# Output projection of a hybrid decoder block: eight quarter products replaced by seven half products, with their sums made by transfers

## The chip, the core and the metric

The kernel runs on one core of one Trainium2 chip. The metric is the device time of one execution in microseconds (us), the median of several runs. All tiles are float32; matrix products are made from pairs of a rounded high part and a low remainder, three matmuls for one product of tiles.

The engines are named as the profile names them: PE (matmuls; PEld is its weight load), DVE (the vector engine), ACT (the scalar engine), POOL (GpSimd) and SP (the queue from which nearly all transfers are issued). Each engine takes its instructions in order.

## What is computed

One decoder block over a sequence of 1024 tokens with a model width of 1024. The part that the change rewrites is the output projection `y @ w_out`:

```
y = sigmoid(g_a) * (o_a @ w_o_swa) + sigmoid(g_b) * (o_b @ w_o_mla)
x = x + y @ w_out
h = rmsnorm(x, ffn_norm_g)
x = x + (silu(h @ w_gate) * (h @ w_up)) @ w_down
return rmsnorm(x, final_norm_g)
```

Here `o_a` and `o_b` are the outputs of a windowed attention and of a causal attention with eight heads each.

## The kernel before

The kernel runs through stages, each bound to PE. First come the norm and the input projections, the windowed attention with the gate products, and the causal attention (64 steps of one head and one block of 128 queries). In step t, PE makes the scores of step t + 2 and the transposes of the probabilities of step t; between the two, DVE masks (L1204), ACT takes the exponent into `p` (L1205) and POOL inverts the denominator `denb` (L1206) and scales `p` (L1207). In gaps of this order PE makes the product with `w_o_swa` (`mix_a`, tiles `oA`).

Then `mix_b` makes `o_b @ w_o_mla` into PSUM tiles `oB`, eight blocks of 128 columns of y with two halves of the sequence each. For each, ACT takes the sigmoids, POOL multiplies the first gate with its product (L1442), DVE multiplies `oB` with the second gate (L1428), adds the two into the tile `sg` (L180, `add`), and `split` (L163 on ACT, L166 on DVE) makes the high part `yh` and the low part `yl` in four pairs of tiles ("quads").

The output projection follows (loop `seg`). It runs over four quarters of the output: rows 0 to 511 left, rows 0 to 511 right, rows 512 to 1023 right, rows 512 to 1023 left. A quarter has four blocks of 128 rows, a block takes eight tiles of 128 along the inner dimension, and each of these takes the three matmuls of `mm3` (L172, L173, L174) with 512 columns into a PSUM tile `xo`. DVE adds the PSUM tile to the residual `x`. `w_out` is loaded in units of 128 x 1024 (`wr`) and split into `wv` (or `wh`, `wl`), four units for a quarter, the right half once for two quarters.

Of the rows that are complete, ACT takes the sum of squares (L1652), POOL the factor `rstd` (L311, L314), and DVE the scaled rows `xn` (L1657). PE transposes them (`to_h`, tiles `tp`), and ACT and DVE make from them the operands `b11`, `b21`, `b22`, `t1` to `t4` of the feed-forward stage, which already uses a scheme of seven half products for one of eight (class `Seven`: of two matrices cut into quarters, sums of quarters are formed, seven products of halves are made instead of eight, and the results are combined; `Seven.mix` and `Seven.prep` make its weight sums). Its products go to PSUM tiles `fa` and `fb`. The last stage is the down projection (`fd`).

Who stands where in an engine's queue is decided by the program: under `tc.manual_schedule` the named engines keep the order in which the code is written; outside it a scheduler orders them. SBUF tiles of 4 KB a partition come from a pool `U` of 21, those of 8 KB from a pool `V` of 17; PSUM tiles come from two pools of four banks (`P1` and `PX`). A tile that is asked for waits until the oldest of its pool is free.

Of the kernel before, what the change touches and what calls it, by code (L numbers as in the profile page):

```python
# [89 lines left out]
def hybrid_block_kernel(  # L90
# [208 lines left out]
    for dp in range(4):  # L299
        plain(("oa", dp), w_o_swa[dp], (P, 4, 256), True)  # L300
    for dp in (2, 0, 3, 1):
        plain(("ob", dp), w_o_mla[dp], (P, 4, 256))
    OUT0 = (2, 0, 3, 1)
    for r, hf in enumerate((0, 1, 0)):
        for j in (range(4) if r else OUT0):
            plain(("out", r, j), w_out[hf, j], (P, 2, 512), (r, j) != (2, 3))


# [722 lines left out]
    for it in range(N_SW):  # L1031
        if it + 2 < N_SW:
            sw_q(it + 2)
        gate_step()
        if it + 1 < N_SW:
            sw_qT(it + 1)
        sw[it].pop("norm")()
        gate_step()
# [245 lines left out]
    def mix_a(dc, sh, c0, n, ps=None):  # L1284
# [3 lines left out]
        if (sh, c0) == (0, 0):  # L1288
            if dc < 4:
# [9 lines left out]
        if c0 + n == 4:  # L1299
            nc.scalar.copy(ar[dc][:, half(sh)], oa_ps.pop((dc, sh)))  # L1300
            if sh == 1 and dc < 4:
                nc.sync.dma_start(ar_d[dc], ar.pop(dc))
# [16 lines left out]
    DCS = (4, 5, 0, 1, 6, 7, 2, 3)  # L1319

    def load_sigs(dc):
        for i in (dc, 8 + dc):
            load_sig(i)
        if dc < 4:
            ar[dc] = U("ar")
            nc.sync.dma_start(ar[dc], ar_d[dc])
# [35 lines left out]
    units = [(u // 2, u % 2, c) for u in range(16 - 3) for c in (0, 2)]  # L1362
# [4 lines left out]
    pvq = []  # L1367
    for t in range(NT):
# [20 lines left out]
        if t == NT - 1:  # L1389
            mix_a(13 // 2, 13 % 2, 0, 4, PX("oA"))  # L1390
        transposes(t)
        held[0] = True
# [5 lines left out]
        if t + 6 in w_at or t == 0:  # L1398
            st.load_to(st.index[("oa", w_at.get(t + 6, 0))])
# [6 lines left out]
        if e in (2, 6):  # L1406
            st.load_to(st.index[("ob", 2 if e == 2 else 0)])
        if e == 6:
            st.conv_to(st.index[("ob", 2)])
        held[0] = False  # L1410
    rest = [(i // 2, i % 2) for i in range(14, 16)]
# [6 lines left out]

    def mix_b(dc, i):
# [3 lines left out]
        ga, gb = gate.pop(dc), gate.pop(8 + dc)  # L1423
        for sh in range(2):
# [4 lines left out]
            if i == 7:  # L1429
                add(ga[:, cs], ga[:, cs], gb[:, cs], nc.vector)  # L1430
                split(*hT(dc, cs), ga[:, cs])
        for sh in range(2 if i < 7 else 0):
            cs = half(sh)
            add(ga[:, cs], ga[:, cs], gb[:, cs], nc.vector)
            split(*hT(dc, cs), ga[:, cs])
# [14 lines left out]
    st.conv_to(st.index[("ob", 0)])  # L1450
    new_quads("y")
    for i, dc in enumerate(DCS):
        if i in (1, 2):
            st.load_to(st.index[("ob", (3, 1)[i - 1])])
        if 2 <= i < 6:
            st.load_to(st.index[("out", 0, OUT0[i - 2])])
# [4 lines left out]
        if i + 1 < 8:  # L1461
            sigmoids(DCS[i + 1])
        mix_b(dc, i)
        if i in (1, 3):
            st.conv_to(st.index[("ob", (3, 1)[i // 2])])
        if i >= 4:
            st.conv_to(st.index[("out", 0, OUT0[i - 4])])

# [3 lines left out]
    x2 = {}  # L1472
# [3 lines left out]
    def to_h(xn, b):  # L1476
# [3 lines left out]
        for kh in range(2):  # L1480
            ps = PX("tp", (P, 4, P))
# [16 lines left out]
        t23 = U("t23", F32, (P, 2, 4, P))  # L1498
        sub(r[:, 0], pss[0], r[:, 0], nc.vector)
        nc.scalar.copy(t23[:, 1], pss[0])  # L1500
        sub(t23[:, 0], pss[1], r[:, 0], nc.vector)
        nc.scalar.copy(hq["t2"][0][:, :, blk(c)], t23[:, 0])
        sub(r[:, 1], r[:, 1], t23[:, 0], nc.vector)
        late.append((c, r))

        def rest():
            sub(t23[:, 1], pss[1], t23[:, 1], nc.vector)
            nc.scalar.copy(hq["b22"][0][:, :, blk(c)], pss[1])
            nc.scalar.copy(hq["t3"][0][:, :, blk(c)], t23[:, 1])  # L1509
            for name, src in (("t2", t23[:, 0]), ("b22", pss[1]), ("t3", t23[:, 1])):  # L1510
                hi, lo = hq[name]
                sub(lo[:, :, blk(c)], src, hi[:, :, blk(c)].bitcast(F32), nc.vector)
# [102 lines left out]

    in_order = tc.manual_schedule(engines={engines.PE, engines.DVE, engines.Activation, engines.Pool})
    prev = None
    late_parts = []
    for seg, (sh, hf) in enumerate(((0, 0), (0, 1), (1, 1), (1, 0))):
        if seg == 3:  # L1620
            in_order.__enter__()
        if seg in (0, 1, 3):
            r = {0: 0, 1: 1, 3: 2}[seg]
            wo2 = [st.get(("out", r, j)) for j in range(4)]
        hs = half(hf)
        for b in range(4 * sh, 4 * sh + 4):
            if seg in (0, 2):
                x2[b] = load_x(b)
            if (seg, b) == (2, 4):
                ffn.load_part(0, 0)  # L1630
            if (seg, b) == (2, 6):
                ffn.load_part(0, 1)
            if (seg, b) == (2, 7):
                ffn.mix(0)
            if seg == 0 and b < 2:
                if b == 0:
                    xo2 = [P1("xo") for _ in range(2)]
                    for ks in (DCS[:6], DCS[6:]):
                        for u in range(2):
                            mm3(xo2[u], [(hT(k, blk(u)), (wo2[k // 2][0][:, k % 2], wo2[k // 2][1][:, k % 2])) for k in ks],  # L1640
                                ks[0] == DCS[0], ks[0] != DCS[0])
                ps = xo2[b]
            else:
# [249 lines left out]
```

## Time and profile before

| what | value |
|---|---|
| time of the kernel, median of 3 runs | 1337.02 us (1336.59 to 1338.35) |
| time of the profiled execution | 1336.93 us |
| its span, first to last instruction | 1335.1 us |
| PE busy | 1323.6 us, 99% |
| DVE, ACT, POOL busy | 904.6, 636.5, 567.0 us |
| granted clock of PE over the span | 0.998 |

The span lies 1.8 us below the time of its own execution, which lies 0.1 us below the median. The profile's times are counted from the span's start. The first matmul of the output projection starts at 603.9 us, its last at 696.1 us.

### The profile page before, as it was taken

To read this page: it belongs to the slowest core of one execution; us is meant where nothing else is said; L and a number is where in the kernel's file an instruction comes from. 1 tells how busy PE (TensorE), PEld (TensorE's weight loads), DVE (VectorE), ACT (ScalarE), POOL (GpSimd) and SP (SyncE) were. 2 spreads that over 40 slices of the span, in tenths; PEclk is the share of its full clock that TensorE was granted. 3 is DMA by queue.
4 is the path that set the end of the run, shared out by engine and by line. 5 is a ranking of instruction groups with operands and counts; after the bars stand their busy time and mean duration, and the time that the engine had idled before them with its cause. 6 is when DMAs were issued, how large, how long until landed. Compare 5 with 4: busy or idle time off the path is not lost. (4 is left out here: it accounts for less than half of the span.)

```text
span 1335.1 us, 19045 instructions
## 1 busy us (share of the span) xinstructions
PE 1323.6 (99%) x6564; PEld 1115.3 (84%) x6564; DVE 904.6 (68%) x1471; ACT 636.5 (48%) x1291; POOL 567.0 (42%) x614
## 2 busy tenths in 40 slices
PE   9999999999999999999999999999999999999997
PEld 6899888888888889888887888888888888888886
DVE  7868777776767767696469766666665654664862
ACT  7434676675556766753335323322233233644443
POOL 2115556552325554451131765755666541022521
PEclk9999999999999999999999999999999999999999
DMA  9454322335575530681532354534443425996504
GB/s 376 154 188 163 108 104 83 119 115 193 160 246 151 111 95 17 252 291 56 222 129 91 143 182 172 200 133 181 181 162 142 169 95 191 386 381 223 174 16 142
DMA packets 85311, 223.61 MB, mean 167 GB/s; under 512 B 9632, under 2 KB 16288, under 8 KB 84128
## 3 DMA queue, kind: packets, MB, share of 16 engines
q1 hardware_dynamic: 83776, 220.05, 47.1%
q10 hardware_dynamic: 1440, 2.36, 0.5%
q8 instruction: 52, 0.85, 0.3%
q14 instruction: 43, 0.35, 0.1%
HBM read 151.72 MB, written 70.12 MB: 166 GB/s over the span
## 5 line engine op out<-in xcount | busy, mean ns | idle before, releaser
L166 DVE TENSOR_TENSOR wl<-wr,wl 128x512 fp32r<-128x512 f32 x150 | 148.7, 1015 | 71.2 <-ACT wl L163 70.9
L166 DVE TENSOR_TENSOR lrv<-lr,lrv 128x1024 fp32r<-128x1024 f32 x77 | 105.1, 1396 | 49.0 <-ACT lrv L163 46.4
L163 ACT CAST lrv<-lr 128x1024 fp32r<-128x1024 f32 x77 | 80.1, 1052 | 95.6 <-PE fd L174 69.5
L172 PE MATMUL fd<-lrv 128*128 128x512 f32 x308 | 119.8, 389 | 0.0
L173 PE MATMUL fd<-lrv 128*128 128x512 f32 x308 | 119.8, 389 | 0.0
L174 PE MATMUL fd<-lrv 128*128 128x512 f32 x308 | 119.8, 389 | 0.0
L177 POOL TENSOR_TENSOR wr<-wr,sm 128x512 f32<-128x512 f32 (+1 forms) x38 | 45.8, 1213 | 162.6 <-DVE wl L166 136.2
L163 ACT CAST wl<-wr 128x512 fp32r<-128x512 f32 x150 | 87.0, 623 | 1.4 <-DVE wr L835 1.1
L1206 POOL TENSOR_TENSOR denb<-denb,neg_one 128x1 f32<-128x1 f32 x64 | 40.1, 627 | 96.2 <-ACT p L1205 84.4
L166 DVE TENSOR_TENSOR wl<-sm,wl 128x512 fp32r<-128x512 f32 x60 | 48.2, 829 | 42.2 <-ACT wl L163 42.1
L173 PEld LDWEIGHTS fd<-lrv 128*128 128x128 f32 x308 | 57.8, 188 | 12.1
L174 PEld LDWEIGHTS fd<-lrv 128*128 128x128 f32 x308 | 57.8, 188 | 12.0
L172 PEld LDWEIGHTS fd<-lrv 128*128 128x128 f32 x308 | 57.8, 188 | 11.9
L311 POOL TENSOR_SCALAR ms<-ss 128x1 f32<-128x1 f32 x32 | 8.9, 277 | 138.0 <-ACT xn L1652 61.1
L1205 ACT ACTIVATE p<-scb,nmb 128x384 f32<-128x384 f32 (+3 forms) x64 | 47.8, 747 | 33.3 <-DVE nmb L1204 25.6
L166 DVE TENSOR_TENSOR ptl<-pTb,pth 128x512 fp32r<-128x512 f32 (+2 forms) x96 | 50.5, 551 | 16.6 <-ACT pth L163 16.2
L1204 DVE CUSTOM_DVE_ANT_0 scb<-scb,mask 128x384 f32<-128x384 f32 (+3 forms) x64 | 48.5, 760 | 15.0 <-PE scb L1196 13.0
L1537 ACT ACTIVATE act<-sm 128x512 f32<-128x512 f32 x11 | 7.0, 632 | 104.4 <-DVE sm L180 104.4
L1207 POOL TENSOR_SCALAR p<-p,denb 128x384 f32<-128x384 f32 (+3 forms) x64 | 48.0, 749 | 6.3
L1537 ACT ACTIVATE act<-pu 128x512 f32<-128x512 f32 x22 | 13.9, 633 | 70.6 <-DVE pu L180 70.6
L163 ACT CAST pth<-pTb 128x512 fp32r<-128x512 f32 (+2 forms) x96 | 43.5, 482 | 8.5 <-PE pTb L1221 7.5
L172 PE MATMUL fb<-t2h,wl 128*128 128x512 f32 x120 | 47.4, 395 | 0.0
(356 smaller groups left out, 4319.1 us busy)
## 6 DMA issues: line engine op xcount, KB each, us to landing
lr<-la_d SPq DMA_DIRECT2D x77, 256.0 KB, 5.4
wr<-in_w_gate_dram SPq DMA_DIRECT2D x22, 512.0 KB, 4.2
wr<-in_w_up_dram SPq DMA_DIRECT2D x22, 512.0 KB, 5.0
wd<-in_w_down_dram SPq DMA_DIRECT2D x22, 512.0 KB, 6.9
rb_d<-wd SPq DMA_DIRECT2D x22, 512.0 KB, 2.7
la_d<-sd SPq DMA_DIRECT2D x22, 512.0 KB, 5.7
lr<-rb_d SPq DMA_DIRECT2D x44, 256.0 KB, 5.4
lr<-in_w_down_dram SPq DMA_DIRECT2D x33, 256.0 KB, 5.4
```

What stands on the lines that cost most here:

```text
L163: i = nc.scalar.copy(hi, src)
L166: (eng or nc.vector).tensor_tensor(lo, src, hi.bitcast(F32), op=ALU.subtract)
L172: nc.tensor.matmul(ps, ah, bh, start=first and i == 0, stop=False, skip_group_check=go_on)
L173: nc.tensor.matmul(ps, ah, bl, start=False, stop=False, skip_group_check=go_on)
L174: nc.tensor.matmul(ps, al, bh, start=False, stop=last and i == n - 1, skip_group_check=go_on)
L177: eng.tensor_tensor(out, a, b, op=ALU.subtract)
L311: nc.gpsimd.tensor_scalar(ms, ss, 1.0 / width, EPS, op0=ALU.mult, op1=ALU.add)
L1204: nc.vector.tensor_tensor_reduce(s_, s_, m_, 1.0, -NEG, op0=ALU.add, op1=ALU.min, accum_out=nm)
L1205: nc.scalar.activation(p_, s_, AF.Exp, scale=-1.0, bias=nm, accum_out=den)
L1206: nc.gpsimd.tensor_tensor(den, den, neg_one[:, 0:1], op=ALU.pow)
L1207: nc.gpsimd.tensor_scalar(p[:, 0:w], p[:, 0:w], den, 0.0, op0=ALU.mult, op1=ALU.add)
L1537: nc.scalar.activation(dst, src, AF.Silu)
```

## The change

The output projection becomes seven products of halves. A product takes four blocks of 128 rows, four inner tiles and three matmuls. Its left operands are the quarters of y or sums of them, its right operands quarters of `w_out` or sums of them. Numbers of the products: 1, 2 and 3 take plain weights; 5, 7, 6 and 4 take the sums `t1`, `t3`, `t2`, `t4`.

- **Sums of weights.** Four scratch tensors in memory (`wt_d`) are filled during the attention stages: four copies from memory to memory are issued on SP, and four transfers that add to their destination (`accum_op`) on POOL, each 1 MB (`out_sums`). The copies and two sums stand at fixed steps of the causal attention (`OUT_AT`).
- **Sums of y.** 16 transfers from SBUF to SBUF that add to their destination, 128 x 512 each, are issued on POOL (`left_sum`). The parts of y for the second half of the inner dimension are kept with the sign turned (L1491 of the new file). Splits of the sums follow (`split_left`), 16 of them beside 12 of the plain quarters in `mix_b`; before there were 16 in all.
- **Order.** The products run in the order 1, 2, 5, then 6 and 3 in turns, then 7, 3, 4 in turns with the transposes. From there PE, DVE, ACT and POOL keep the written order up to the feed-forward stage. Each block of each product is taken from PSUM by DVE: 28 times, before 16. A bank is used by several products one after the other (`go_on`), and DVE reads it in between.
- **Feed-forward start.** In `to_h`, the fourth sum of a tile (`r[:, 1]`) goes from DVE to POOL, and sums that read PSUM stand ahead of the splits. The loads of the first feed-forward weights, the splits of them and the late splits get new places.
- **Names and places.** The order of column blocks `DCS` and of the `mix_a` units changes, so that the blocks 4 to 7 and not 0 to 3 pass through memory (`ar_d`). The split `w_o_mla` now lies in the pool `V`.

The core of the diff:

```diff
+    W_SRC = {1: w_out[0, 0:2], 2: w_out[0, 2:4], 3: w_out[1, 2:4], 5: wt_d[0], 6: wt_d[1], 7: wt_d[2], 4: wt_d[3]}
...
+    def more(dst, src, **kw):
+        return nc.gpsimd.dma_start(dst, src, accum_op=ALU.add, **kw)
...
+        def copy(dst, src):
+            tc.keep_in_program_order(nc.sync.dma_start(dst, src))
+
+        def sum_(dst, src):
+            tc.keep_in_program_order(more(dst, src, max_dma_last_dim=4096))
...
+    OUT_AT = {40: 1, 43: 2, 47: 3, 50: 4, 54: 5, 58: 6}
...
+    def left_sum(n, *ks):
+        for k in ks:
+            a_lo, a_hi, b_lo, b_hi = (ya[k + d][:, half(sh)] for d in (0, 4) for sh in range(2))
+            more(*{0: (b_hi, a_hi), 1: (a_hi, a_lo), 2: (a_lo, b_hi), 3: (b_lo, a_lo)}[n])
+
+    def split_left(q, *ks):
...
+        d, sh = {5: (4, 1), 7: (0, 1), 6: (0, 0), 3: (4, 0)}[q]
+        for k in ks:
+            split(left[q][0][:, k], left[q][1][:, k], ya[k + d][:, half(sh)])
...
+    SUMS = {6: [(0, 0), (0, 1)], 7: [(0, 2), (1, 0), (1, 1)]}
...
-        sub(r[:, 1], r[:, 1], t23[:, 0], nc.vector)
+        sub(r[:, 1], r[:, 1], t23[:, 0], nc.gpsimd)
...
+    def xo(q, b):
+        if q in (1, 2, 5):
+            bank[("B" if q == 1 else "A", b)] = (PX if q == 1 else P1)("xo")
+        ps = bank[("B" if q in (1, 6, 7, 4) else "A", b)]
...
+        mm3(ps, [((lh[:, k, blk(b)], ll[:, k, blk(b)]), (w[k // 2][0][:, k % 2], w[k // 2][1][:, k % 2]))
+                 for k in range(4)], first=q in (1, 2, 5), go_on=q in (6, 7, 4, 3))
+        x_ = x2[b if q in (1, 2, 6, 3) else 4 + b][:, lo if q in (1, 2, 4) else hi]
+        if q in (1, 5, 7):
+            add(x_, ps, x_, nc.vector)
+        else:
+            sub(x_, x_, ps, nc.vector)
...
+    for n, k in ((0, 3), (1, 2), (2, 0), (2, 1), (1, 3), (2, 2), (3, 0), (3, 1), (2, 3), (3, 2), (3, 3)):
+        left_sum(n, k)
...
+    xo(2, 0)
+    split_left(5, 0, 1)
...
+    xo(5, 2)
+    split_left(6, 2, 3)
+    xo(5, 3)
+    conv(3, 1)
+    split_left(3, 0, 1)
+    ahead(7, 1)
+    xo(6, 0)
```

Three places show what this does to the queues. The first is POOL in the causal attention, around step 43 of 64, in the kernel before. `denb` is the denominator of a step and `p` its probabilities; the columns tell the step (896 is step 42, 1024 step 43, 128 step 44).

```order
L1206 TENSOR_TENSOR denb_5766<-denb_5766,neg_one 128x1
L1207 TENSOR_SCALAR p_5765<-p_5765,denb_5766 128x896
L1206 TENSOR_TENSOR denb_5793<-denb_5793,neg_one 128x1
L1207 TENSOR_SCALAR p_5792<-p_5792,denb_5793 128x1024
L1206 TENSOR_TENSOR denb_5819<-denb_5819,neg_one 128x1
L1207 TENSOR_SCALAR p_5818<-p_5818,denb_5819 128x128
L1206 TENSOR_TENSOR denb_5869<-denb_5869,neg_one 128x1
L1207 TENSOR_SCALAR p_5868<-p_5868,denb_5869 128x256
```

In the changed kernel the same place reads so:

```order
L1257 TENSOR_TENSOR denb_5772<-denb_5772,neg_one 128x1
L1258 TENSOR_SCALAR p_5771<-p_5771,denb_5772 128x896
L328 DMA wt_d_115<-in_w_out_dram 256x1024
L1257 TENSOR_TENSOR denb_5800<-denb_5800,neg_one 128x1
L1257 TENSOR_TENSOR denb_5826<-denb_5826,neg_one 128x1
L1258 TENSOR_SCALAR p_5799<-p_5799,denb_5800 128x1024
L1258 TENSOR_SCALAR p_5825<-p_5825,denb_5826 128x128
L1257 TENSOR_TENSOR denb_5876<-denb_5876,neg_one 128x1
L1258 TENSOR_SCALAR p_5875<-p_5875,denb_5876 128x256
L328 DMA wt_d_117<-in_w_out_dram 256x1024
```

The transfer that adds 1 MB in memory stands ahead of step 43's denominator, and the denominator of step 44 has moved ahead of the scaling of step 43.

The second place is POOL between the last gate products of `mix_b` and the first factor `rstd` of the output projection. Before, `rstd` follows the gate products directly:

```order
L1442 TENSOR_TENSOR sg_6821<-ar_6825,sg_6821 128x512 x2
L1442 TENSOR_TENSOR sg_6870<-ar_6874,sg_6870 128x512 x2
L311 TENSOR_SCALAR ms_7160<-ss_7158 128x1
L314 TENSOR_TENSOR rstd_7162<-ms_7160,neg_half 128x1
L311 TENSOR_SCALAR ms_7195<-ss_7193 128x1
L314 TENSOR_TENSOR rstd_7197<-ms_7195,neg_half 128x1
```

Now the 16 adding transfers stand there (`sg` are the tiles of y; the columns are 512). The transfers use eight semaphores in turn, and `DMASW4` is that of the first of them: the fourth waits for the first, the fifth for the second, the seventh for the third, and so on.

```order
L1526 TENSOR_TENSOR sg_6869<-ar_6873,sg_6869 128x512
L328 DMA sg_6623<-sg_6470 128x512 [waits DVE_49]
L328 DMA sg_6681<-sg_6603 128x512 [waits DVE_49]
L328 DMA sg_6825<-sg_6730 128x512 [waits DVE_49]
L328 DMA sg_6470<-sg_6470 128x512 [waits DMASW4_49]
L328 DMA sg_6603<-sg_6603 128x512 [waits DMASW5_49,DMASW0_49]
L328 DMA sg_6869<-sg_6778 128x512 [waits DMASW1_49,DVE_49]
L328 DMA sg_6730<-sg_6730 128x512 [waits DMASW6_49,DMASW2_49]
L328 DMA sg_6470<-sg_6623 128x512 [waits DMASW7_49,DMASW3_49]
L328 DMA sg_6603<-sg_6681 128x512 [waits DMASW0_49]
L328 DMA sg_6778<-sg_6778 128x512 [waits DMASW1_49]
L328 DMA sg_6730<-sg_6825 128x512 [waits DMASW2_49]
```

Five more of them follow up to `rstd`. What moved: the first factor `rstd` now stands behind 16 transfers, most of which wait for an earlier one. The sixth writes the last part of product 5's left operand, the fourteenth that of product 6 and the sixteenth that of product 3; the tenth waits for the sixth, the fourteenth for the tenth and the sixteenth for the fourteenth.

The third place is DVE in the output projection. Before, DVE has one addition and one split of a weight unit for a block of eight inner tiles:

```order
L180 TENSOR_TENSOR x_7057<-xo_7002,x_7057 128x512
L166 TENSOR_TENSOR wv_7062<-wr_7060,wv_7062 128x1024
L180 TENSOR_TENSOR x_7065<-xo_7067,x_7065 128x512
L166 TENSOR_TENSOR wv_7095<-wr_7093,wv_7095 128x1024
L180 TENSOR_TENSOR x_7098<-xo_7100,x_7098 128x512
L166 TENSOR_TENSOR wv_7128<-wr_7126,wv_7128 128x1024
```

Now, in the same stage, at products 2 and 5, it reads PSUM twice as often in PE time, and splits sums of y between:

```order
L177 TENSOR_TENSOR x_6999<-x_6999,xo_7094 128x512
L166 TENSOR_TENSOR yl_7109<-sg_6623,yh_7108 128x512
L166 TENSOR_TENSOR yl_7109<-sg_6681,yh_7108 128x512
L177 TENSOR_TENSOR x_7001<-x_7001,xo_7118 128x512
L166 TENSOR_TENSOR yl_7109<-sg_6825,yh_7108 128x512
L166 TENSOR_TENSOR yl_7109<-sg_6869,yh_7108 128x512
L177 TENSOR_TENSOR x_7003<-x_7003,xo_7140 128x512
L316 SCALAR_TENSOR_TENSOR wv_7154<-wr_7056,wv_7154 128x1024
L166 TENSOR_TENSOR yl_7158<-sg_6470,yh_7157 128x512
L177 TENSOR_TENSOR x_7005<-x_7005,xo_7163 128x512
L316 SCALAR_TENSOR_TENSOR wv_7177<-wr_7075,wv_7177 128x1024
L166 TENSOR_TENSOR yl_7158<-sg_6603,yh_7157 128x512
```

The rows `yl` have moved here from `mix_b` or are new, and each waits for its sum.

More of the change, by code (lines that the diff above doesn't have):

```diff
@@ L1670, in hybrid_block_kernel @@
+    ffn.prep_to(2)
+    xo(7, 0)
+    norm_b(2)
+    to_h_of(1)
+    xo(3, 3)
+    norm_a(3)
+    ffn.mix(0)
+    ffn.prep_to(3)
+    xo(7, 1)
+    norm_b(3)
+    to_h_of(2)
+    xo(4, 0)
+    norm_a(4)
+    ffn.prep_to(5)
+    xo(7, 2)
+    norm_b(4)
+    to_h_of(3)
+    xo(4, 1)
+    norm_a(5)
+    xo(7, 3)
+    norm_b(5)
+    xo(4, 2)
+    norm_a(6)
+    to_h_of(4)
+    xo(4, 3)
+    norm_a(7)
+    norm_b(6)
+    lowers.pop(4)()
+    for kh in range(2):
+        ffn.load_part(1, kh)
     ffn.n_ahead = 1
```

327 lines of the change are left out of this document (215 added, 112 removed).

## The prediction

> **What bounds the kernel now.** The first view is the page's table of busy times, with the granted clock of TensorE in 40 slices.
>
> ```profile
> PE 1323.6 (99%) x6564; PEld 1115.3 (84%) x6564; DVE 904.6 (68%) x1471; ACT 636.5 (48%) x1291; POOL 567.0 (42%) x614
> PEclk9999999999999999999999999999999999999999
> ```
>
> PE is busy 99% of the span, at full clock, so time goes only with PE's work or with new waits of PE. The second view is PE's waits from 400 to 720 us, the stretch that the change touches; columns are total, times and longest, in us.
>
> ```profile
> PE scb L1194 <- ACT p L1205: 0.9, 2, 0.6
> PE oA L173 <- DVE wv L166: 0.5, 1, 0.5
> PE fa L172 <- ACT wl L163: 0.4, 1, 0.4
> ```
>
> The longest is 0.6 us, and none lies in the output projection. The third view is that stage by time (604 to 697 us): busy time of each engine, then the granted clock, the DMA share and GB/s, with the 24 us of `mix_b` ahead of it.
>
> ```profile
> 580.00:604.00 24.00, 24.00 (x108) 19.87 (x107) 23.62 (x27) 14.63 (x18) 11.57 (x7) 1.00 0.85 311
> 604.00:620.00 16.00, 16.00 (x73) 13.23 (x72) 13.29 (x17) 8.29 (x11) 3.44 (x2) 1.00 0.06 26
> 620.00:640.00 20.00, 20.00 (x94) 16.65 (x93) 6.73 (x8) 3.71 (x8) 1.48 (x4) 1.00 0.13 53
> 640.00:660.00 20.00, 20.00 (x102) 16.80 (x101) 9.39 (x12) 6.81 (x15) 1.48 (x4) 1.00 0.50 188
> ```
>
> PE is full throughout. From 620 to 660 us DVE is busy 16.1 of 40 us, POOL 3.0 and the transfers next to nothing up to 640: that is the room. DVE is full only just ahead, 23.62 of 24 us.
>
> **The change, part by part.** *The product.* Eight inner tiles, 16 blocks and three matmuls are 384; seven products of four tiles, four blocks and three are 336. The order of PE agrees: 48 go, transposes stay. Two neighbours of the timeline give the price of one:
>
> ```profile
> 603.87 0.39 PE L172 MATMUL xo<-wv,yh 128*128 128x512 f32 x1
> 604.10 0.39 PE L173 MATMUL xo<-wv,yh 128*128 128x512 f32 x1
> L172 PE MATMUL xo<-wv,yh 128*128 128x512 f32 x120 | 47.2, 394 | 0.0
> ```
>
> They start 0.227 us apart over the stage (92.2 us hold 384 and the transposes), though one spans 0.39 from start to end. 48 x 0.227 = **-10.9 us**; a block of 12 takes 2.72 us, a product 10.9.
>
> *Sums of weights.* In memory 8 MB are copied or added during the attention. From 480 to 560 us the transfers have room:
>
> ```profile
> 480.00:560.00 80.00, 79.48 (x518) 70.51 (x517) 56.60 (x119) 56.51 (x127) 37.66 (x55) 1.00 0.31 102
> ```
>
> A share of 0.31 hides the volume; if it were full, loads of the keys would come late. What counts is POOL's time for the issue. The trace has no issue on POOL and no adding transfer; the nearest rows are SP's issues, the longest of them here:
>
> ```profile
> 590.19 0.33 SPq L238 DMA_DIRECT2D wr<-in_w_out_dram  x1
> 598.92 1.16 SPq L238 DMA_DIRECT2D wr<-in_w_out_dram  x1
> L1442 POOL TENSOR_TENSOR sg<-ar,sg 128x512 f32<-128x512 f32 x16 | 27.1, 1714 | 32.3 <-ACT sg L1277 27.2 <-DVE sg L1428 5.1
> ```
>
> I bound it by 0.33 us and by 1.71, POOL's own sum of such a tile, and take 1.3, near the longest issue. At step 43 the issue stands ahead of the denominator, and that of step 44 has moved ahead of the scaling:
>
> ```profile
> 496.83 1.02 POOL L1207 TENSOR_SCALAR p<-p,denb 128x896 f32<-128x896 f32 x1
> 498.25 0.55 POOL L1206 TENSOR_TENSOR denb<-denb,neg_one 128x1 f32<-128x1 f32 x1 [0.40 <-ACT p L1205]
> 498.89 1.12 POOL L1207 TENSOR_SCALAR p<-p,denb 128x1024 f32<-128x1024 f32 x1
> 500.54 1.04 PE L1221 MATMUL pTb<-ident,p 128*128 128x128 f32 x8
> 505.30 0.55 POOL L1206 TENSOR_TENSOR denb<-denb,neg_one 128x1 f32<-128x1 f32 x1 [1.16 <-ACT p L1205]
> ```
>
> POOL is free at 497.85, issues until 499.15, inverts twice until 500.3, and scales until 501.5, where PE wants it at 500.54: **+1.0**, at 0.33 nothing, at 1.71 +1.4. The other sums in memory fall into idle times of 1 us or more, such as the one at 505.30: nothing.
>
> *Sums of y.* Their first condition is POOL's last gate product:
>
> ```profile
> 606.64 3.44 POOL L1442 TENSOR_TENSOR sg<-ar,sg 128x512 f32<-128x512 f32 x2 [4.71 <-ACT sg L1277]
> ```
>
> It ends at 610.1, 6.2 us after the projection begins (603.9); times below count from there. The longest chain of waits in POOL's queue is transfer 1, 4, then 5 and 6 behind it in the queue, 10, 14, 16: seven issues and five landings, so the last lands at 6.2 + 7 x issue + 5 x landing. Products 1, 2 and 5 take PE until 32.6, then come two blocks of product 6 and one of product 3, and PE wants the sixteenth, split, at about 36.5. With 1.3 the limit is a landing of 4.2 us. Rows of landings (KB, then median us from issue):
>
> ```profile
> x_d<-x SPq DMA_DIRECT2D x8, 512.0 KB, 2.6
> ar_d<-ar SPq DMA_DIRECT2D x1, 512.0 KB, 3.5
> lr<-la_d SPq DMA_DIRECT2D x77, 256.0 KB, 5.4
> ffng<-in_ffn_g_dram SPq DMA_DIRECT2D x1, 512.0 KB, 8.2
> ```
>
> The bounds are 2.6 and 8.2. The 2.6 comes from this same stage, where little else moves; the 5.4 from loads between many others. The transfer is half as large but reads two sources, so I take 4.0, between the nearest two: the last lands at 35.3, in time. **0**, with DVE idle for a while at the sixth. The Trainium skill, *DMA: Bandwidth & Descriptors* (Anatomy of one DMA, SWDGE), fits 2.0 us plus bytes at 436 GB/s for a transfer issued on GpSimd; for 256 KB that is an estimate of 2.6 us, and the last would land at 28.3. No run here shows such a transfer yet, and the fit is not for adding ones.
>
> *DVE and ACT.* DVE takes PSUM 28 times for 16, splits 28 tiles for 16, and 14 weight units for 12. Rows, by stage:
>
> ```profile
> L180 DVE TENSOR_TENSOR x<-xo,x 128x512 f32<-128x512 f32 x15 | 10.3, 689 | 21.7 <-PE xo L174 20.9 <-DMA x<-in_x_dram 0.8
> L166 DVE TENSOR_TENSOR wv<-wr,wv 128x1024 fp32r<-128x1024 f32 x8 | 10.1, 1257 | 4.7 <-ACT wv L163 4.7
> L166 DVE TENSOR_TENSOR yl<-sg,yh 128x512 fp32r<-128x512 f32 x16 | 14.0, 879 | 2.5 <-ACT yh L163 2.1
> L163 ACT CAST yh<-sg 128x512 fp32r<-128x512 f32 x16 | 9.9, 618 | 20.9 <-DVE sg L180 20.9
> ```
>
> A product now asks of DVE, in 10.9 us of PE, four takes (2.8), up to seven splits of y (6.2 at 0.88) and two weight units (2.5): 11.4 at product 5, 10.5 at product 2, 8.0 at product 1. So it is full, but `mix_b` loses four splits of y to it (-3.5 us of DVE there), which is lead. ACT needs 0.62 for each split and is free. I cost three starts of products on fresh splits (5, 6, 3) at the 0.5 us of the longest such wait in the second view: **+1.5**, from 0 (the projection of before waits for nothing) to one block each, 8.2.
>
> *The start of the feed-forward stage.* PE waits there 0.39 us for ACT and 0.18 for the unit before:
>
> ```profile
> 715.05 0.50 PE L172 MATMUL fa<-b21h,wl 128*128 128x512 f32 x1 [0.39 <-ACT wl L163]
> 718.52 0.50 PE L172 MATMUL fa<-b21h,wl 128*128 128x512 f32 x1 [0.18 <-ACT pu L812]
> ```
>
> Taking the sums ahead of the splits can save these 0.6 us; the fourth sum on POOL, a two-input operation of 1.71 for DVE's 0.68 or so, can cost 1.0 once. I take **0**, between -0.6 and +1.0.
>
> *Sum*: 1335.1 - 10.9 + 1.0 + 1.5 = 1326.7 of span. The profiled execution was 1336.93, 1.8 above its span, and the median lies 0.1 above that: 1326.7 + 1.9 = **1328.6 us**. Without the 1.5 it is 1327.1, from which the rivals count.
>
> **The rivals.** *The sums of y come late.* PE, DVE and the splits then wait in a row for transfers, and every us beyond 36.5 is PE's. A landing of 5.4 puts the last at 6.2 + 9.1 + 27.0 = 42.3: 5.8 late, 1332.9. Both upper bounds, 1.71 and 8.2, give 59.2: 22.7 late, 1349.8. This is the rival on the other side: it gives the whole gain back at 5 x landing = 36.5 + 9.9 - 15.3, a landing of 6.2, and is slower by over 0.2% (2.7 us; a measurement of this kernel tells no less from no change) beyond 6.8 us. For it speak the 5.4 and 8.2 and that each adding transfer waits for the landing of another; against it the 2.6 us in the same stage, where the transfers' share was 0.06 to 0.13.
>
> *DVE becomes the bound.* Beside a POOL operation DVE's operations with two SBUF operands are longer:
>
> ```profile
> 592.05 3.54 POOL L1442 TENSOR_TENSOR sg<-ar,sg 128x512 f32<-128x512 f32 x2 [2.44 <-ACT sg L1277]
> 592.42 2.01 DVE L166 TENSOR_TENSOR wv<-wr,wv 128x1024 fp32r<-128x1024 f32 x1
> 594.36 1.77 DVE L166 TENSOR_TENSOR yl<-sg,yh 128x512 fp32r<-128x512 f32 x1
> 598.40 0.68 DVE L166 TENSOR_TENSOR yl<-sg,yh 128x512 fp32r<-128x512 f32 x1
> ```
>
> If POOL's issuing does the same, the ten blocks from product 2's second to product 6's second (27.2 us of PE) hold 16 splits at 1.77, five weight units at 2.01 and ten takes at 0.69: 45.3 us of DVE. Less one block of lead, PE loses 15.4: 1342.5. It begins to cost when such a split takes 1.06 us. Against it: between POOL's operations the same split takes 0.68, and an issue moves no tile through POOL. The Trainium skill, *SBUF — State Buffer* (Who interferes with whom), says that a DVE operation with two SBUF inputs contends only with a GpSimd operation that reads SBUF, and, as an inference, that descriptor generation needs the write side, which such an operation leaves free; by that rule the splits stay at 0.68 and this rival falls away. The rows above agree with its first half; none here shows the second.
>
> *Part comes back*: a stall of DVE at the sixth transfer or a late weight unit that costs two blocks more, 1331 to 1334. *The change does not do what it says*: the order shows 48 matmuls fewer, so only a PE that waits as long could hide them.
>
> **How the numbers follow.** Forecast, 1325.5 to 1331, 0.50, with 1328.6 the likeliest. Below 1325.5, if no term but the first counts and the start of the feed-forward stage gains: 0.05. Part lost, 1331 to 1334.3: 0.16. Sums late or DVE behind by most of the gain, 1334.3 to 1339.7: 0.13. Slower, 0.16: sums landing beyond 6.8 us 0.10, DVE bound 0.06. So faster 0.71, same 0.13, slower 0.16. The range leaves out the 0.05 below and 0.15 above: 1325.5 to 1340.5.
>
> **What would show it.** Right: 336 matmuls `xo` at 0.227 us; the last adding transfer landing before 36 us after the first of them; splits `yl` in the projection at 0.7 to 0.9 us; one PE wait near 1 us at step 43 for POOL's scaling. Wrong: PE waiting at products 5, 6 or 3 for ACT's casts `yh`, which wait for a transfer (sums late), or for DVE's splits at over 1.06 us (DVE bound); POOL's issues above 1.7 us, which would also lengthen the wait at step 43 and at the other three places.

## The result: 3.8 us faster, where 8.4 were forecast

| | median us | from, to | runs |
|---|---|---|---|
| before | 1337.22 | 1336.59, 1338.35 | 8 |
| changed | 1333.42 | 1331.59, 1337.89 | 8 |

The ratio is 0.9973 (95% interval 0.9962 to 0.9985), a gain of 2.0 to 5.1 us. The forecast was 1328.6; what came is its case "part comes back". The page of the changed kernel, PE to POOL:

```profile
span 1332.5 us, 19056 instructions
PE 1316.1 (99%) x6516; PEld 1105.5 (83%) x6516; DVE 923.7 (69%) x1493; ACT 644.4 (48%) x1306; POOL 592.7 (44%) x638
```

There are 48 matmuls less (6564 before). PE's busy time falls by 7.5 us, less than the 10.9 that they took, because PE's waits are in part so short that the modelled ends of the matmuls cover them. So I read starts, not busy times. The waits of PE from 490 to 760 us in the changed kernel, where the kernel before had two of 0.4 and 0.2 us behind 600 us:

```profile
PE fb L172 <- DVE pu L180: 1.1, 1, 1.1
PE fa L172 <- ACT pu L861: 0.7, 1, 0.7
PE pTb L1272 <- POOL p L1258: 0.5, 1, 0.5
PE tp L1575 <- DVE xn L1742: 0.5, 1, 0.5
PE oA L174 <- DVE wv L166: 0.3, 1, 0.3
PE xo L172 <- ACT yh L163: 0.3, 1, 0.3
PE xo L173 <- DVE wv L166: 0.2, 1, 0.2
```

All but that of `oA` are new, and most name DVE, or ACT behind DVE.

**A measure that leaves chance out.** Ahead of the causal attention both kernels hold the same rows but for two transfers, yet the first score matmul starts anywhere between 376.5 and 381.0 us (the last experiments show where). I therefore compare the *stretch* from that matmul to the last `fa` matmul of the feed-forward stage. Its two ends in the kernel before, the changed one, and the run "all three" below:

```profile
376.90 0.34 PE L1194 MATMUL scb<-kT,qT 96*128 96x384 f32 x1
...
1118.27 0.39 PE L174 MATMUL fa<-b22h,wl 128*128 128x512 f32 x1
```

```profile
379.48 0.34 PE L1245 MATMUL scb<-kT,qT 96*128 96x384 f32 x1
...
1115.51 0.39 PE L174 MATMUL fa<-b22h,wl 128*128 128x512 f32 x1
```

```profile
379.43 0.34 PE L1245 MATMUL scb<-kT,qT 96*128 96x384 f32 x1
...
1109.87 0.39 PE L174 MATMUL fa<-b22h,wl 128*128 128x512 f32 x1
```

That makes 741.4, 736.0 and 730.4 us: the change brings 5.3 us here. (Two more traces of the kernel before gave 741.1 and 741.2, a second one of the changed kernel 736.3.) Behind the stretch both kernels take 209.4 to 209.5 us to their last matmul.

**Where the 10.9 went.** I matched the matmuls of the two traces in order and noted where the distance between partners jumps. The changed kernel loses 0.8 us at step 43 of the attention, 0.9 in `mix_b`, 0.9 at the start of product 2 (618.9 to 621.3), 0.8 in product 6 (643.3), 1.9 at 696 to 702, 0.3 at 717 and 1.4 at 750; it saves the 1.3 that PE waited at 715 to 719 before. -10.9 + 7.0 - 1.3 = -5.2. The rows behind the larger ones follow.

At the end of `mix_b` (PE is done with it at 608.0) DVE goes through column halves: the product with the gate (L1503), the sum (L1491), then the low part (L166), for which it waits for ACT's high part each time:

```profile
609.24 0.68 DVE L1503 TENSOR_TENSOR sg<-oB,sg 128x512 f32<-128x512 f32 x1
610.02 0.69 DVE L1491 SCALAR_TENSOR_TENSOR sg<-sg,sg 128x512 f32<-128x512 f32 x1
611.40 0.69 DVE L166 TENSOR_TENSOR yl<-sg,yh 128x512 fp32r<-128x512 f32 x1 [0.69 <-ACT yh L163]
612.01 0.68 DVE L1503 TENSOR_TENSOR sg<-oB,sg 128x512 f32<-128x512 f32 x1
...
617.62 0.68 DVE L180 TENSOR_TENSOR x<-xo,x 128x512 f32<-128x512 f32 x1
618.22 1.22 DVE L166 TENSOR_TENSOR wv<-wr,wv 128x1024 fp32r<-128x1024 f32 x1
```

One half takes 2.8 us, 0.7 of it idle, and DVE takes the first block of product 1 only at 617.6, when PE is nearly through with all four. The first weight unit of product 2 is split from 618.2 on, just when PE asks for it. The sums of y wait for the same splits (third transfer, `<-DVE yl`). POOL's row and DVE's splits from 608 to 660:

```profile
L328 POOL DMA_DIRECT2D sg<-sg x16 | 14.1, 899 | 21.8 <-issue 13.1 <-DMA sg<-sg 6.7 <-DVE yl L166 1.9
L166 DVE TENSOR_TENSOR yl<-sg,yh 128x512 fp32r<-128x512 f32 x20 | 13.6, 700 | 6.8 <-ACT yh L163 6.8
```

At the start of the feed-forward stage DVE stands still for POOL's factor, with a PSUM tile and two splits queued behind, and later PE waits for DVE (first fence DVE, second PE):

```profile
683.77 1.28 DVE L1742 SCALAR_TENSOR_TENSOR xn<-x,rstd,ffng 128x1024 f32<-128x1024 f32 x1 [1.49 <-POOL rstd L363]
684.98 0.68 DVE L166 TENSOR_TENSOR b11l<-tp,b11h 128x512 fp32r<-128x512 f32 x1
...
689.12 1.28 DVE L1742 SCALAR_TENSOR_TENSOR xn<-x,rstd,ffng 128x1024 f32<-128x1024 f32 x1 [1.67 <-POOL rstd L363]
690.32 0.68 DVE L177 TENSOR_TENSOR x<-x,xo 128x512 f32<-128x512 f32 x1
```

```profile
697.40 1.09 PE L1575 MATMUL tp<-ident,xn 128*128 128x128 f32 x8 [0.48 <-DVE xn L1742]
...
702.22 0.50 PE L172 MATMUL fa<-b21h,wl 128*128 128x512 f32 x1 [0.73 <-ACT pu L861]
...
751.15 0.47 PE L172 MATMUL fb<-t3h,wl 128*128 128x512 f32 x1 [1.12 <-DVE pu L180]
```

### The profile page after: what moved, and what is told of

It reads as the page before. It is cut to its first block, busy times and chain, and to the rows that moved or that the text cites. A ratio compares the mean times of both kernels' runs of the same rounds, so it can differ in the third digit from the quotient of the medians.

```text
span 1332.5 us, 19056 instructions
## 1 busy us (share of the span) xinstructions
PE 1316.1 (99%) x6516; PEld 1105.5 (83%) x6516; DVE 923.7 (69%) x1493; ACT 644.4 (48%) x1306; POOL 592.7 (44%) x638
## 5 line engine op out<-in xcount | busy, mean ns | idle before, releaser
L166 DVE TENSOR_TENSOR wl<-wr,wl 128x512 fp32r<-128x512 f32 x150 | 149.4, 1019 | 73.8 <-ACT wl L163 73.3
L166 DVE TENSOR_TENSOR lrv<-lr,lrv 128x1024 fp32r<-128x1024 f32 x77 | 105.1, 1396 | 50.2 <-ACT lrv L163 44.6
L166 DVE TENSOR_TENSOR wl<-sm,wl 128x512 fp32r<-128x512 f32 x60 | 51.7, 885 | 43.1 <-ACT wl L163 43.0
L166 DVE TENSOR_TENSOR ptl<-pTb,pth 128x512 fp32r<-128x512 f32 (+2 forms) x96 | 50.5, 552 | 16.8 <-ACT pth L163 16.5
L172 PE MATMUL fb<-t3h,wl 128*128 128x512 f32 x120 | 47.4, 395 | 1.1 <-DVE pu L180 1.1
L172 PE MATMUL fa<-t1h,wl 128*128 128x512 f32 x120 | 47.2, 393 | 1.2 <-ACT wl L163 1.2
```

Source lines behind the costliest of these rows:

```text
L166: (eng or nc.vector).tensor_tensor(lo, src, hi.bitcast(F32), op=ALU.subtract)
L172: nc.tensor.matmul(ps, ah, bh, start=first and i == 0, stop=False, skip_group_check=go_on)
```

## The experiments

The kernel before (ratios are to its runs beside each variant) and the changed one gave stretches of 741.4 and 736.0. Stretches are of one trace each. Two waits of PE differ in size between runs whose edits don't touch them, and the stretch holds both: the one in product 6 (0.5 to 2.1 us with the old order of `mix_b`, by starts, against the run without sums of y) and one near 686 us (0 to 1.0). All variants but the last three start from the changed kernel.

| run | edit | stretch us | median us | ratio (interval) |
|---|---|---|---|---|
| after_again | none | 736.3 | 1334.27 | 0.9972 (0.9963 to 0.9981) |
| e1_sum_at_42 | first sum in memory two steps later | 738.6 | 1336.11 | 0.9993 (0.9983 to 1.0002) |
| e7_sum_at_35 | the same, one head earlier | 736.8 | 1333.54, one run | |
| e2_dve_order | DVE in written order in `mix_b` | 737.5 | 1334.70 | 0.9979 (0.9970 to 0.9989) |
| e8_order_conv | and weight units earlier | 734.1 | 1330.61 | 0.9940 (0.9923 to 0.9956) |
| e3_fourth_dve | fourth sum on DVE | 737.5 | 1334.15 | 0.9975 (0.9964 to 0.9985) |
| e4_old_to_h | old order in `to_h` | 740.9 | 1338.11 | 1.0006 (0.9996 to 1.0015) |
| e5_low_pool | low part of t3 on POOL | 738.6 | 1334.52, one run | |
| e9_wd_later | sums of w_down later | 736.6 | 1333.04, one run | |
| e6_no_y_sums | no sums of y | 734.7 | 1334.49, one run | |
| e10_norm_order | scalings behind ready work | 735.0 | 1330.68 | 0.9948 (0.9934 to 0.9961) |
| e11_all_three | e7, e8 and e10 | 730.4 | 1328.53 | 0.9931 (0.9919 to 0.9944) |
| e13_ahead_3 | e11, three units ahead | 729.4 | 1326.59 | 0.9913 (0.9899 to 0.9928) |
| e14_before_memsums | before, with sums in memory | 741.9 | 1338.48 | 1.0006 (0.9997 to 1.0015) |
| before_b | before again | 741.1 | 1338.29, one run | |
| before_c | before again | 741.2 | 1338.21, one run | |

### Step 43: where the first sum in memory stands

```diff
-    OUT_AT = {40: 1, 43: 2, ...
+    OUT_AT = {42: 1, 43: 2, ...    # e1_sum_at_42
+    OUT_AT = {35: 1, 43: 2, ...    # e7_sum_at_35
```

> The first adding transfer in memory is issued two steps later, behind the scaling of step 44 (128 columns), not ahead of step 43's (1024). I read the stretch from the first score matmul of the causal attention to the last fa matmul, which leaves out what differs between two executions earlier: 741.4 us before, 736.0 in the changed kernel. Theory: PE lost 0.78 us at step 43 only because the issue stood ahead of a wide step; the loss goes and the stretch becomes 735.2. Rival: an issue of 1.1 us costs PE wherever it stands; then a loss of 0.5 to 1.0 shows at step 45 or 46 and the stretch stays 736.0.

> The first adding transfer in memory goes one head earlier, to the same place within the head as the second one (behind the step of 256 columns), where the second costs PE nothing in the changed kernel. Theory: the loss at an issue depends on the next step's width; the 0.67 to 0.78 us at step 43 go, attention from first score to first oB falls from 184.1 to 183.4, the stretch to 735.3. Rival: each further issue costs about 0.7 to 2 (as behind step 44), 184.1 or more.

The loss at step 43 went in both. In the first a larger one came in its place: PE lost 2.1 us near 511, and POOL shows why.

```profile
500.58 1.12 POOL L328 DMA_DIRECT2D wt_d<-in_w_out_dram  x1
...
503.32 0.48 POOL L1258 TENSOR_SCALAR p<-p,denb 128x256 f32<-128x256 f32 x1
508.75 0.52 SPq L337 DMA_DIRECT2D wt_d<-wt_d  x1
509.00 0.98 POOL L328 DMA_DIRECT2D wt_d<-in_w_out_dram  x1 [5.21 <-issue]
509.68 0.91 POOL L1257 TENSOR_TENSOR denb<-denb,neg_one 128x1 f32<-128x1 f32 x1
```

The second transfer began 8.4 us after the first, and POOL stood still for 5.2 us with no semaphore to explain it. What ended that is the landing of the first: the copy at 508.75 waits for the same sum, and POOL issues 0.25 us behind it. In the changed kernel the second transfer began at 508.57, 0.26 us after the first had landed and 8.2 us after it began, and PE lost nothing there: POOL had waited 1.35 us. So both readings fell short: the issue itself is 1.1 us and costs PE by its place (with the first one a head earlier, attention took 183.4 us, as before), but an adding transfer of 1 MB also holds the next one back until it has landed. The stretch of e7_sum_at_35 was 736.8, above what the theory gave, though the loss at step 43 was gone: the waits in product 6 and near 686 were 0.5 and 0.9 us longer in this one run.

### `mix_b`: DVE's order

```diff
-    pool_order = tc.manual_schedule(engines={engines.Pool})
+    pool_order = tc.manual_schedule(engines={engines.Pool, engines.DVE})   # e2, e8
...
+        if i >= 6:                                        # e8: moved up
+            st.conv_to(st.index[("out", 1, i % 2)])
         mix_b(dc, i)
...
-        if i >= 6:
-            st.conv_to(st.index[("out", 1, i % 2)])
```

> DVE keeps the written order in mix_b too: both products with the gate, both sums, then both splits of a column block, so that it doesn't stand idle for ACT's high part between (0.69 to 0.75 us four times after 608 us in the changed kernel). Theory: DVE's lag at the start of the projection comes from these waits; PE's losses at the start of product 2 (0.88 us, 618.9 to 621.3) and in mix_b (0.86) go, the transfers that wait for DVE's splits start earlier and the 0.80 in product 6 goes too; the stretch falls from 736.0 to 733.5 to 734.5. Rival: DVE is late by its load alone (21.4 of 24 us busy), so the order changes nothing there (736.0), or holds PSUM longer and costs up to 1 us in mix_b (737).

> DVE keeps the written order in mix_b as in the run before, and the two weight units of product 1 are split ahead of the last two column blocks, since there a unit behind them cost 3.2 us at the start of the projection. Theory: what PE loses in mix_b (0.88), at product 2 (0.88) and in product 6 (0.80) is DVE idling for ACT within mix_b; all three go, mix_b takes 43.5 us, and the stretch falls to 733.4 to 734.2. Rival: DVE's load alone: the losses move to product 1 or 2 and the stretch stays 735.5 to 736.5.

In the first, `mix_b` fell from 44.4 to 43.5 us, as in the kernel before, and the waits at product 2 and in product 6 went; but a weight unit of product 1 now stood behind the last column block, and PE stood for it:

```profile
607.50 0.39 PE L172 MATMUL xo<-wv,yh 128*128 128x512 f32 x1
610.90 0.79 PE L173 MATMUL xo<-wv,yh 128*128 128x512 f32 x1 [3.02 <-DVE wv L166]
611.49 0.63 PE L174 MATMUL xo<-wv,yl 128*128 128x512 f32 x1
611.92 0.63 PE L172 MATMUL xo<-wv,yh 128*128 128x512 f32 x1
```

With the two units moved up, nothing in `mix_b` and products 1 to 6 made PE wait, and all three losses were gone. DVE in that run:

```profile
608.12 1.28 DVE L1503 TENSOR_TENSOR sg<-oB,sg 128x512 f32<-128x512 f32 x2
609.32 1.29 DVE L1491 SCALAR_TENSOR_TENSOR sg<-sg,sg 128x512 f32<-128x512 f32 x2
610.74 1.29 DVE L166 TENSOR_TENSOR yl<-sg,yh 128x512 fp32r<-128x512 f32 x2
611.95 0.68 DVE L180 TENSOR_TENSOR x<-xo,x 128x512 f32<-128x512 f32 x1
```

The same operations, two by two, need no wait, and DVE reaches product 1 at 611.95, 4.0 us after PE began the projection; in the changed kernel it took 9.6. The theory held, load as the cause did not. The kernel before has the same waits for ACT (0.74 and 0.69 us before its last two splits) at no cost: a block of its first product keeps PE busy for 5.4 us, here one of 2.72.

### The start of the feed-forward stage

```diff
-        sub(r[:, 1], r[:, 1], t23[:, 0], nc.gpsimd)
+        sub(r[:, 1], r[:, 1], t23[:, 0], nc.vector)                  # e3_fourth_dve
...
-        nc.scalar.copy(b22[0], pss[1])                               # e4_old_to_h: to rest()
-        sub(t23[:, 1], pss[1], t23[:, 1], nc.vector)                 # likewise
-        sub(b22[1], pss[1], b22[0].bitcast(F32), nc.vector)          # likewise
...
-            sub(t3[1], t23[:, 1], t3[0].bitcast(F32), nc.vector)
+            sub(t3[1], t23[:, 1], t3[0].bitcast(F32), nc.gpsimd)     # e5_low_pool
```

> The fourth sum of a tile goes back from POOL to DVE, all else as in the changed kernel. Theory: DVE bounds PE from 690 to 750 us (busy 22.1 of 23 us from 697 on), so four more operations of 0.69 us there cost 0.7 to 2.8: the stretch rises from 736.0 to between 736.7 and 738.8. Rival: POOL's operation of 1.3 us is what the others wait for, and the stretch stays or falls by up to 1 us.

> In to_h the third sum and the high part of b22 stand behind the splits again as in the kernel before, the fourth sum stays on POOL. Theory (DVE bounds the start of the feed-forward stage by its load): the order alone moves the stretch by less than 0.5 us, 735.5 to 736.5. Rival: the new order causes the waits of PE at 696.5 and 701.1 us (1.9 us in all), and the stretch falls by 1 to 2 us, to 734 to 735.

> The low part of t3 of the last four tiles goes from DVE to POOL (four operations of 0.69 us less on DVE), all else as in the changed kernel. Theory: DVE's load bounds PE from 690 to 750 us, as the way back showed (four more operations: +1.44 us of the stretch); the stretch falls from 736.0 to 734.5 to 735.5. Rival: these operations have two operands in SBUF, so on POOL they lengthen DVE's own ones beside them (0.69 to 1.78 us) and delay the operand; the stretch rises by 0.5 to 1.5.

The fourth sum on DVE cost 1.4 us of stretch, within what the theory gave, but 0.5 of it lies in product 6 and near 686, and the median was no longer than the changed kernel's; PE's wait for `xn` rose from 0.5 to 1.1. The old order of `to_h` did what neither reading expected: 4.8 us, nearly all that the change brings. Of these, 3.6 lie behind 690 us, and 1.2 in the two waits that differ from run to run; the median rose by 3.8 to 4.7. Its waits of PE from 600 to 760 us:

```profile
PE fa L172 <- ACT pu L861: 3.4, 3, 1.9
PE fb L172 <- DVE pu L180: 1.5, 2, 1.1
PE xo L172 <- DVE x L180: 0.7, 1, 0.7
PE fb L173 <- DVE t2l L177: 0.5, 1, 0.5
```

Moving the low part of t3 to POOL brought nothing: a new loss of 1.1 us came near 722, behind operations of DVE that POOL's lengthen, as the rival said. POOL and DVE of that run:

```profile
712.30 3.45 POOL L177 TENSOR_TENSOR t3l<-t,t3h 128x512 fp32r<-128x512 f32 x2
715.72 3.44 POOL L177 TENSOR_TENSOR wr<-wr,sm 128x512 f32<-128x512 f32 x2
```

```profile
714.53 1.77 DVE L177 TENSOR_TENSOR t2l<-t,t2h 128x512 fp32r<-128x512 f32 x1
716.23 3.47 DVE L166 TENSOR_TENSOR wl<-wr,wl 128x512 fp32r<-128x512 f32 x2
```

Its stretch, 738.6, also holds 1.0 us more in product 6 than the changed kernel's, which the edit doesn't touch.

Then DVE's waits instead of its load:

```diff
     xo(7, 2)
-    norm_b(4)
     to_h_of(3)
+    norm_b(4)
...
     xo(7, 3)
-    norm_b(5)
     xo(4, 2)
+    norm_b(5)                                                        # e10_norm_order
```

> Two scalings of rows (norm_b of the fifth and sixth block) stand behind work that is ready on DVE, where in the changed kernel DVE waits 1.49 and 1.67 us for POOL's factor (at 683.8 and 689.1 us) while a PSUM tile and two splits stand behind. Theory: DVE's queue bounds the start of the feed-forward stage, by its waits as much as by its load; PE's waits at 695 to 701 us (1.8 us in all) go, and with DVE less behind the 1.28 at 749 shrinks; the stretch falls from 736.0 to 733.5 to 734.5. Rival: load alone; the waits only move, 735.5 to 736.5.

The waits of PE from 690 to 720 are all gone, and the one near 749 stays, against the theory. The stretch, 735.0, lies above what the theory gave because product 6 lost 1.3 us more this time:

```profile
PE xo L172 <- ACT yh L163: 1.5, 1, 1.5
PE fb L172 <- DVE pu L180: 1.1, 1, 1.1
PE xo L173 <- DVE wv L166: 0.2, 1, 0.2
```

DVE waited 0.30 and 0.36 us for the factor, where it had waited 1.49 and 1.67. So the load of DVE stayed the same, and the two waits had cost PE the 1.9 us at 696 to 702 and the 0.3 at 717.

### The wait near 749 us

> The four sums of w_down on POOL, and their loads, come later in the feed-forward stage's first pair, all else as in the changed kernel. Theory: the 1.28 us that PE loses at 749.6 us come from DVE's operations that these sums lengthen (1.77 for 0.68 us between 734 and 742), while DVE is behind; the loss goes or halves and the stretch falls to 734.7 to 735.4. Rival: DVE is behind by its own load, and the loss stays at 1.3.

The edit (the sums of w_down issued at another unit, `3 if j == 0`) moved them by only 2.3 us (736.8 for 735.6, with POOL 1.2 us earlier in that run just ahead), since they now waited for their load; DVE's operations beside them still took 1.7 us and the wait stayed at 1.3. This run decides nothing.

### Without the sums of y

The 16 transfers were left out (`left_sum` does nothing).

> The changed kernel without the 16 adding transfers of y (so products 5, 6, 7 and 3 take plain parts of y and the output isn't the reference's); splits and products stay. Theory: the sums cost PE only the wait in product 6 (0.4 to 1.4 us in the runs so far) and DVE's lag from mix_b sets the rest; that wait goes, the 0.88 in mix_b and 0.88 at product 2 stay, the stretch becomes 735.0 to 735.8. Rival: the lag of the sums spreads to the start of the feed-forward stage, whose waits (1.7 us at 695 to 701, 1.28 at 749) shrink too, and the stretch falls to 733 or lower.

The wait in product 6 went, and so did 0.6 us at 696; what is lost in `mix_b`, at product 2, at 701 and at 749 stayed. The late sums cost PE some 1.4 us in all (one run), a little further on than the theory had it.

### All three, and again

> DVE's written order with the early weight units in mix_b (measured -1.9 in the stretch), the first sum in memory a head earlier (-0.7) and the scalings behind ready work. If the three losses are separate, as theory has it, the stretch is 734.1 - 0.7 - 1.5 to 2.5 = 731 to 732 and the time some 1327 to 1329 us. Rival: DVE's load is one budget, and what one saves another spends: 733 to 734, 1330 us.

> The kernel with all three edits, and behind the written order the feed-forward stage splits three units ahead and not four. Theory: the 1.29 us that PE still loses near 744 us come from splits that stand ahead of a PSUM take on DVE; with fewer of them ahead the loss goes and the stretch falls from 730.4 to 729.1 to 729.6. Rival: the loss comes from what DVE is behind already, and it stays or moves on (730.4 or more, since splits also come later).

The three edits together gave 730.4, 0.6 below what the theory gave; some 0.3 of that is the wait near 686, which the 734.1 of e8_order_conv holds and this run does not. Its only wait from 600 to 760 us is the one near 744:

```profile
PE fb L172 <- DVE pu L180: 1.1, 1, 1.1
```

With `ffn.n_ahead = 3` in place of 4 behind the written order this one is gone too, with 729.4 within what the theory gave: splits for later units stood ahead of the PSUM tile that PE waited for. That kernel is the fastest of all, 1326.59 us (1325.32 to 1328.13).

### What lies ahead of the stretch

> The changed kernel once more, beside the others. Theory: what differs ahead of the first score matmul (379.5 us in the changed kernel's profile, 376.9 before, 376.5 to 380.2 in its variants) is chance between executions, since the queues there hold the same rows but for two transfers; so its time is 1332 to 1335 and its stretch 736.0 to 737. Rival: the two copies in memory or the program's size cost 1 to 2.5 us there each time, and the first score is again above 378.5.

> The kernel before with the sums of weights in memory added (four copies on SP, four adding transfers on POOL, at the changed kernel's places) and not used. Theory: they cost what POOL's issue at the wide step costs, 0.7 us, and nothing else: stretch 741.4 + 0.7 = 742.1 and time 0.7 us over the kernel before. Rival: their scratch tensors or queues also cost the 1 to 2 us that the changed kernel and its variants seem to lose ahead of the first score: time 1.7 to 2.7 over before.

> The kernel before once more, for its profile. If what differs ahead of the first score matmul is chance of loads that land late, its first score lies anywhere in the 376.5 to 381.0 us of the changed kernel and its variants, and its stretch is 741.4 within 0.3. If the changed kernel costs time there, it lies again at 376.9 or below.

> The same once more: a third sample of the first score and the stretch of the kernel before, with the same two readings.

The first score came at 376.9, 378.6 and 378.4 us in the kernel before, and between 376.5 and 381.0 in the changed kernel and its variants (14 traces, mean 378.3). The distance to the first trace of before jumps at three places. In five traces PE gets through only 4 or 5 matmuls from 6.2 to 9.2 us, in the other 13 through 7 to 9, and all that follows comes 1.9 to 2.3 us later: before_b, e2, e11, e13 and e14, so both kernels have that by chance. The other two are PE's waits near 117 us (for a load) and near 152 us (for a split of weights behind a load). Together they cost between -0.3 and 4.2 us against that first trace, 0.9 in the mean of the 14, and 0.2 in the mean of the kernel before (with e14). In the changed kernel's trace the wait near 152 ends at 153.4, ahead of any transfer that the change adds (the copies, from 154.3). So most of the spread is chance; a cost of up to a us there is not excluded. The sums in memory alone cost 0.7 us of stretch by the same issue at step 43; their 1.2 us of time are not clear of nothing (interval -0.4 to +2.0).

One difference stays open: the medians of the changed kernel lie 3.0 and 3.8 us below those of before, its stretches 4.9 to 5.4. Eleven medians of several runs can be set beside a stretch (the changed kernel twice, eight variants, the sums in memory alone): nine gained less on the kernel before than their stretch did, by 0.5 to 2.0 us, and two gained 0.4 and 0.5 more. Part of it may be that the waits in product 6 and near 686 differ from run to run, part a cost ahead of the first score. The runs don't settle it.

## Why the forecast missed, step by step

The four costs of the sum came to 1.0 + 0 + 1.5 + 0 = 2.5 us; the stretch shows 0.7 + 0.8 + 1.8 + 2.3 = 5.6. Of the 4.6 us by which the median missed (3.8 for 8.4) these are 3.1. The other 1.5 lie outside the stretch or between one run and the next, and stay open.

- **The product, -10.9: right.** Its products of 48 matmuls start 10.88 us apart wherever nothing waits. With the waits taken out (all three), the stretch is 10.8 us below the mean of the three traces of before (741.2); the 1.3 us that this run still loses near 744 and the 1.3 that it saves at 715 to 719 cancel.
- **Sums of weights, +1.0: right in kind, 0.7 to 0.8.** POOL's issue took 0.93 to 1.12 us for 1.3. That a transfer holds up the next until it has landed was in none of the bounds, and cost nothing by luck of the places.
- **Sums of y, 0: 0.8 at product 6 (0.5 to 2.1 in other runs with the old order of `mix_b`, nothing with the new one).** Two errors met. The landing took 5.9 us in the median and not 4.0, by which the last would have come 8 us late; but the first transfer began 0.7 us after the projection, not 6.2, because POOL's last gate product ended earlier. The last landed 39.8 us after the projection began, later than the 36 given as a sign of being right, and PE did not wait for it: it waited for the fourteenth, in product 6. The chain of waits also left one out. From the eighth to the fifteenth, each transfer began 0.31 us after the landing of the one three places before it, with no semaphore between; so the tenth, whose own condition (the sixth) had landed at 625.5, stood idle for 3.6 us until 630.3, behind the seventh. The estimate by the Trainium skill, *DMA: Bandwidth & Descriptors* (Anatomy of one DMA, SWDGE), 2.6 us, is less than half of the median of the adding transfers here, and below the shortest (3.6).
- **DVE and ACT, +1.5: the size was near, the mechanism failed.** The text counted what DVE does per product and called the four splits that `mix_b` loses "lead" of 3.5 us. DVE had 1.9 us of that lead: it began product 1 at 9.6 us after PE, in the kernel before at 11.5. At each of the last halves it stood 0.7 us waiting for ACT in its own order; with these waits gone it began at 4.0. The cost was 1.8 us, near the 1.5 by luck, since it has another reason and another place (`mix_b` and product 2, not starts on fresh splits), and it made the sums late as well.
- **The start of the feed-forward stage, 0 between -0.6 and +1.0: this is the step that failed most, +2.3.** The gain was there (1.3, the old waits went), but 3.6 came new. The sum looked at two edits in that stage and not at what DVE carries into it, nor at its 3.2 us of waits for POOL's factor right ahead. With these moved and one unit less ahead, 3.3 of the 3.6 were gone. The order of the sums, priced at a gain of at most 0.6, was worth 3.6 to 4.8.
- **The rivals.** "DVE becomes the bound" by POOL's issuing is refuted: beside 16 issues the splits took 0.70 us in the mean, against 1.06 from which it would have cost. By the rule of the Trainium skill, *SBUF — State Buffer* (Who interferes with whom), this rival falls away, and the trace agrees. Where POOL adds tiles (712 to 719 above) the same kind took 1.77, also as that section has it. "The sums come late" was at work, with a small price. "Part comes back" gave the time, and of its two causes the late weight unit was there at product 2 (0.9 us); none named what happened: DVE bound PE by the order of its queue.

The product's gain was thus within reach. That the kernel with three orders mended takes 1328.53 us, the forecast's 1328.6, is luck all the same: its stretch gained 10.8 us, more than the 8.4 of the sum, and its median 2 us less than its stretch.

## What to carry to other kernels

Before a saving on the bound engine is counted in full, walk through the queue of the engine that feeds it, row by row, and add its waits to its work: an engine that is busy 85% of a stretch (DVE from 604 to 640 us) has no room if it stands in order behind another's answer. Put two or more independent halves through each pair of engines (product, product, sum, sum, split, split) and place an operation that needs a chain of other engines behind work that is ready. Where an edit looks like tidying (sums ahead of splits), try it alone: here it was worth 3.6 to 4.8 of 5.3 us.

## What the runs showed of the hardware

- POOL's adding transfers hold one another up until they land, and the profile shows no semaphore for it. Of 256 KB, three were under way at the most: in all 13 runs with the sums of y, the eighth to the fifteenth began 0.31 us after the landing of the one three places before. In the changed kernel ACT's cast below waits for the eleventh, and the fourteenth begins 0.29 us behind it. In this way 13.1 us of the 16 transfers went by in "issue", beside 0.9 us of issue each. Of 1 MB, one was under way: where two stood near each other, the second began 0.26 us after the first had landed, 8.2 to 8.5 us after it began.

```profile
639.39 0.62 ACT L163 CAST yh<-sg 128x512 fp32r<-128x512 f32 x1 [2.72 <-DMA sg<-sg]
639.68 0.87 POOL L328 DMA_DIRECT2D sg<-sg  x1 [1.54 <-issue]
```

- With them under way a busy transfer engine moved less by the profile's count: with the sums of y the share was 1.08 at 278 GB/s, where a share of 0.85 moved 311 in the kernel before.

```profile
620.00:640.00 20.00, 19.93 (x88) 16.13 (x88) 18.00 (x25) 7.32 (x11) 6.44 (x8) 1.00 1.08 278
```

- A stall of 3.2 us cost PE more than itself. In the run with DVE's order alone (PE idle for 3.0 us) the matmuls behind it started 0.427 us apart and not 0.227, five times, and the granted clock was 0.54 for 3.1 us; PE idle for up to 1.9 us (e1_sum_at_42, e4_old_to_h) left it at full speed.

```profile
607.40:610.90 3.50, 0.48 (x3) 0.06 (x1) 3.31 (x5) 3.13 (x5) 0.89 (x1) 0.92 1.08 273
610.90:614.00 3.10, 3.10 (x8) 2.47 (x9) 0.56 (x1) 1.58 (x3) 1.75 (x2) 0.54 1.08 345
```

The Trainium skill, *TensorE: Matmul & The Clock Gate* (Part 1), gives 426.7 ns between matmuls of 512 columns at the lower clock, after an idle window of some 3.4 us; the 0.427 agrees, and here an idle time of 3.0 us was enough (2.3 in e6_no_y_sums, near 152 us, with a granted clock of 0.56 from 154.0 to 157.3).
